# Row pair nine of a decoder layer's second down product as seven block products, and one exchange split eight and eight

## The chip, the cores and the metric

The kernel runs on one core of a Trainium2 chip. The metric is device time in microseconds (us). A core has a matrix engine (TensorE, PE in the profile, with its weight loads as PEld), VectorE (DVE), ScalarE (ACT), GpSimd (POOL) and a sync engine (SP) that only starts transfers. Each engine works through its own queue in order, and the queues wait for each other by semaphores.

## The reference

One layer of a decoder trunk, 256 positions, model width 1024, feed-forward width 2816, all in float32:

```python
h = x + 0.5 * swiglu(rms_norm(x), w_gate1, w_up1, w_down1)
h = h + hybrid_mixer(rms_norm(h), ...)
h = h + 0.5 * swiglu(rms_norm(h), w_gate2, w_up2, w_down2)
out = rms_norm(h)

def swiglu(x, w_gate, w_up, w_down):
    return (jax.nn.silu(x @ w_gate) * (x @ w_up)) @ w_down
```

The mixer projects to queries, keys, values and gates, runs two kinds of attention, gates, merges and projects back. The change touches the last product of each `swiglu` (the down product) and the step from the first feed-forward to the mixer.

## The kernel before

**Products.** Every large product is split into a rounded high part and a rest: `wh`, `wl` for weights, `hth`, `htl` and the like for activations. A unit (line 360) is three matmuls, high times high, high times `wl`, rest times high, of 128x512 outputs each, that gather in one PSUM bank (`mm3`, lines 354 to 358). After each unit one tick of a list of waiting work runs (`Weave`, from line 101), and then `W.pump` (line 229) may issue one further weight split: ScalarE casts to `wh` (L214, or L218 with a gain), VectorE subtracts to `wl` (L215, L219). The raw weights come in 512 KB transfers of two tiles each, issued by SP, into four slots (`load`, line 171); a slot's next transfer is issued after the split that reads it last.

**Lead of the splits.** During a down product `W.ahead` is 9 and ten pairs `wh`, `wl` exist. So beside product number i stands, in the queues, the split of product i + 8. I count products of the second down product from 0 at its first row pair.

**The down product.** The hidden rows, 2816 long, make 22 blocks of 128, and so eleven row pairs. A plain pair (two blocks, two column halves of the weights, two token halves) has four weight tiles and eight units. For pairs one, three, five and seven (`SEVEN`, g = 0, 2, 4, 6) seven block products stand in place of the eight. `seven()` (from line 654) issues them, and they need

- four sums of weight tiles (`T`, `seventh`, line 196, VectorE) beside three raw tiles, so seven splits in place of four;
- four sums of hidden blocks (`cs`, lines 561 to 564, VectorE), split to `c` (a cast on ScalarE, a subtraction on VectorE). `turn_hidden` (line 549) issues these after the exchange that turns the hidden rows around;
- shared results X, Y, Z, V in two two-bank tiles of PSUM beside the blocks' own banks. Once the last such pair is done, `post()` (line 673) adds combinations of them to h: seven operations on VectorE (L677, L683, L685, L689, L694) and a copy on ScalarE (L681). In the code before it is added to the list after pair seven, with a delay of three ticks.

In the second feed-forward the first nine pairs are the head, over all four result blocks; block (1,1) has its own bank. Then the list is flushed, the residual of block (1,1) is added to h, and the tail runs the last four blocks of rows for result block (0,0), (0,1), (1,0) and (1,1), this one in two pieces of 256 columns. After each follows a residual (L650) and a part of the last normalization (`finish`, line 1164: squares L393 on ScalarE, products with the final gain L1177 and L1185, small steps L1181 to L1193 on VectorE and ScalarE, and the output transfers). So the order on all engines is written out by hand here (`ordered`, from block 3 of the second feed-forward on). Between the end of the first down product's head and that place, only TensorE and SP follow the written order, and a planner orders ScalarE, VectorE and GpSimd.

**The exchange of u.** After the first feed-forward's residual of the left half of h, `moved` (line 428) turns it for token half t: VectorE transposes 32x32 blocks (L432), 16 transfers exchange blocks (`exchange`, L510), and after some ticks ScalarE and VectorE split the result to `uh` and `ul` (L387, L388), which the first projection multiplies. The transfers go in turn to three entries, GpSimd, SP, GpSimd, so eleven are on GpSimd and five on SP, three per tick. Between them SP issues weight transfers. GpSimd also computes the row factors of the norm (L403 to L410) behind them.

Of the kernel before, what the change touches and what calls it, by code (L numbers as in the profile page):

```python
# [21 lines left out]
KD = D // P  # L22
FB = FF // 256
KF = FF // P
# [3 lines left out]
NEG = -1e30  # L28
CH = 2
N_TILES = 376  # L30
SEVEN = (0, 2, 4, 6)
W_DOWN = 2 * KF + 3 * len(SEVEN)
W_IN = FB * KD + W_DOWN
W_BR = W_IN + 10 * KD
W_OUT = W_BR + 16
W_FFN2 = W_OUT + 2 * KD
# [101 lines left out]
def _items():  # L138

    out, n = [], 0  # L140

    def plain(count):
        nonlocal n
        out.extend((n + i, None) for i in range(count))
        n += count

    for f in range(2):
        plain(FB * KD)
        for g in range(KF // 2):
            if g in SEVEN:  # L150
                out.extend((n, j) for j in range(7))
                n += 4
            else:
                plain(4)
        if f == 0:
            plain(W_FFN2 - W_IN)
    assert n == N_TILES
    return out
# [88 lines left out]
def hybrid_layer_kernel(ctx, tc, x, xt, pos, g_final, bgate, wstream, out):  # L247
    nc = tc.nc
# [18 lines left out]
    def big(nm, dt=F32R):  # L267
        return work.tile([P, 1024], dt, name=nm, tag="big", bufs=24)

    def wide(nm, w=768):  # L270
        return work.tile([P, w], F32, name=nm, tag="f", bufs=4)
# [9 lines left out]
    first = consts.tile([P, 3 * KD + T], F32, name="first")  # L281
# [3 lines left out]
    def gain(i):  # L285
        for n, (lo, hi) in enumerate(((0, FB * KD), (W_IN, W_BR), (W_FFN2, W_FFN2 + FB * KD))):
            if lo <= i < hi:
                k = (i - lo) % KD
                if n == 0 and i < 2 * KD:
                    k = i // 2  # L290
                if n == 2 and i - lo < 3 * KD:
                    k = (i - lo) // 12 * 4 + (i - lo) % 4
                return gk[:, n * KD + k:n * KD + k + 1]
        return None

    W = Weights(nc, wpool, lambda nm: big(nm, F32), row512, wstream, gain, WB, AHEAD0)
# [57 lines left out]
    def mm3(o, ah, al, w, first, last):  # L354
        wh, wl = w
        nc.tensor.matmul(o, ah, wh, start=first, stop=False)  # L356
        nc.tensor.matmul(o, ah, wl, start=False, stop=False)  # L357
        nc.tensor.matmul(o, al, wh, start=False, stop=last)  # L358

    def unit(o, a, w, first, last):  # L360
        mm3(o, a[0], a[1], w, first, last)
        weave.tick()
        W.pump()
# [48 lines left out]
    class Normed:  # L412
# [15 lines left out]
        def moved(self, c):  # L428

            s = slice(c * 512, c * 512 + 512)  # L430
            q = big(f"{self.nm}q{self.t}{c}", F32)
            nc.vector.transpose(slots(q[:, 0:512], 4), plain(h[self.t][:, s]))  # L432
            yield D_SQUARES
            queues = [nc.gpsimd, nc.sync, nc.gpsimd] if self.nm == "u" else [nc.sync, nc.gpsimd]
            yield from exchange(q[:, 512:1024], q[:, 0:512], 4, queues, 1)
            yield D_EIGHT
            split(plain(self.parts[0][:, s]), plain(self.parts[1][:, s]), slots(q[:, 512:1024], 4))
            self.there.add(c)
# [59 lines left out]
    def slots(q, n):  # L498

        return q[:, 0:n * P].rearrange("p (g s w) -> p s g w", g=4, s=n)  # L500

    def plain(q):
        return q.rearrange("p (s g w) -> p s g w", g=4, w=32)

    def exchange(moved, squares, n, queues, gap):

        w = 32
        for m in range(16):
            i, j = divmod(m, 4)
            queues[m % len(queues)].dma_start(moved[j * w:j * w + w, i * n * w:(i + 1) * n * w],  # L510
                                              squares[i * w:i * w + w, j * n * w:(j + 1) * n * w])
            if m % len(queues) == len(queues) - 1:
                yield gap
# [14 lines left out]
    def ffn(base, xn, nm, on_half, lag, last=False):  # L528


        hts, crossed = {}, {}
        squares = {}

        def hidden(b, t, bank):
            sh = wide(f"sh_{nm}{b}_{t}", 512)
# [13 lines left out]
        def turn_hidden(p, n):  # L549
            moved = big(f"hm_{nm}{p}", F32)  # L550
            yield from exchange(moved, squares[p], n, [nc.gpsimd if p > 3 else nc.sync], D_MOVE)
            yield D_MOVED
            hts[p] = big(f"hth_{nm}{p}"), big(f"htl_{nm}{p}")
            split(plain(hts[p][0][:, 0:n * P]), plain(hts[p][1][:, 0:n * P]), slots(moved, n))
            for g in range(2 * p, 2 * p + 2):
                if g in SEVEN:
                    a11, a21, a12, a22 = (slots(moved, n)[:, g % 2 * 4 + s] for s in range(4))
                    yield D_SUMS
                    raw = wide(f"cs_{nm}{g}", 512)
                    s1, s3, s2, s4 = (plain(raw)[:, s] for s in range(4))  # L560
                    nc.vector.tensor_add(s1, a21, a22)
                    nc.vector.tensor_sub(s3, a11, a21)
                    nc.vector.tensor_sub(s2, s1, a11)
                    nc.vector.tensor_sub(s4, a12, s2)
                    yield D_SUMS
                    both = big(f"c_{nm}{g}")
                    split(both[:, 0:512], both[:, 512:1024], raw)
                    crossed[g] = [[both[:, q * 512 + m * P:q * 512 + (m + 1) * P] for q in range(2)] for m in range(4)]

        for b in range(FB):  # L570
# [5 lines left out]
            if b == 0 and lag == 0:  # L576
                pairs = [two_banks(f"gu_{nm}{c}") for c in range(2)]
                os = [[pair[:, t * 512:t * 512 + 512] for t in range(2)] for pair in pairs]
                for i in range(2 * KD):
                    k, c = divmod(i, 2)  # L580
# [25 lines left out]
            for t, k in lagged(KD, 2) if b > (2 if lag else 1) else ():  # L606
                if k == 0:
                    banks[t] = acc_bank(f"gu_{nm}{b}_{t}")
                i = base + b * KD + k
# [9 lines left out]
        def out_bank(t, c):  # L619
            if (t, c) not in banks:  # L620
                if (t, c) != (1, 1):
                    banks[t, c] = acc_bank(f"dn_{nm}{t}{c}")
                else:
                    banks[t, c] = y_bank(f"dn_{nm}{t}{c}")
            return banks[t, c]

        def down(t, c, k, i, piece=None):

            o = k % 4 * 256 + t * P
            ht = [q[:, o:o + P] for q in hts[k // 4]]  # L630
            w = W.get(i)
            if piece is not None:
                if k == head:
                    banks[piece] = two_banks(f"dn_{nm}p{piece}")
                cols = slice(piece * 256, piece * 256 + 256)
                mm3(banks[piece][:, 0:256], *ht, [q[:, cols] for q in w], k == head, k == KF - 1)
                weave.tick()
                W.pump()
            else:
                first = (t, c) not in started  # L640
                started.add((t, c))
                unit(out_bank(t, c), ht, w, first, k == (head - 1 if last and (t, c) == (1, 1) else KF - 1))

        def residual(t, c, piece=None):
            if piece is None:
# [6 lines left out]
        common, started = {}, set()  # L652

        def seven(g, i):

            def blk(k, t):
                o = k % 4 * 256 + t * P
                return [q[:, o:o + P] for q in hts[k // 4]]

            if not common:  # L660
                for pair in ("XY", "ZV"):
                    both = two_banks(f"dn_{nm}{pair}")
                    common.update(zip(pair, (both[:, 0:512], both[:, 512:1024])))
            s1, s3, s2, s4 = crossed[g]
            for o, a in (("X", blk(2 * g, 0)), ((0, 0), blk(2 * g + 1, 0)), ((0, 1), s4),
                         ("V", s1), ("Z", s3), ("Y", s2), ((1, 0), blk(2 * g + 1, 1))):
                shared, first = o in common, o not in started
                started.add(o)
                unit(common[o] if shared else out_bank(*o), a, W.get(i), first, shared and g == SEVEN[-1])
                W.done(i)  # L670
                i += 1

# [24 lines left out]

        tail = TAILS[2 if last else 1]
        head = KF - tail
        i = base  # L700
        W.ahead = AHEAD_DOWN
        for k in range(head):
            if k // 2 in SEVEN:
                if k % 2:
                    seven(k // 2, i)
                    i += 7
                    if k // 2 == SEVEN[-1]:
                        weave.add(post(), D_POST)
                continue
            for c in range(2):  # L710
                for t in range(2):
                    down(t, c, k, i)
                W.done(i)
                i += 1
# [8 lines left out]
        for t, c in ((0, 0), (0, 1), (1, 0), (1, 1)) if last else ((0, 0), (1, 0), (0, 1), (1, 1)):  # L723
            pieces = (0, 1) if last and (t, c) == (1, 1) else (None,)
            for piece in pieces:
                for k in range(head, KF):
                    i = base + c * tail + k - head
# [118 lines left out]
    def project(bi, evac):  # L846
        banks = {}
        for t, k in lagged(KD, KD if bi == 0 else 2):
            if k == 0:
                banks[t] = acc_bank(f"in{bi}_{t}")  # L850
            i = W_IN + bi * KD + k
            unit(banks[t], un[t].blk(k), W.get(i), k == 0, k == KD - 1)
# [193 lines left out]
    a, b, ys = {}, {}, {}  # L1046
# [52 lines left out]
    for c in range(2):  # L1099
        banks = {}  # L1100
        for t, k in lagged(4, 2):
            if k == 0:
                banks[t] = acc_bank(f"ba{t}{c}")
            i = W_BR + c * 4 + k
# [28 lines left out]
    for t in range(2):  # L1133
        for c in range(2):
            ps = acc_bank(f"bb{t}{c}")
            for k in range(4):
                i = W_BR + 8 + c * 4 + k
# [8 lines left out]
    for c in range(2):  # L1146
        s = slice(c * 512, c * 512 + 512)
        for t in range(2):
            ps = acc_bank(f"wo{t}{c}")
            for k in range(KD):  # L1150
                i = W_OUT + c * KD + k
# [105 lines left out]
```

## Time and profile before

| what | us |
|---|---|
| three runs, median (lowest to highest) | 548.54 (548.23 to 549.52) |
| the profiled execution, its own time | 549.75 |
| its span from first to last instruction | 548.0 |
| TensorE's granted clock, mean | 0.997 of full |
| first matmul of the second down product | 484.15 |
| last matmul | 541.30 |

Busy times of engines are shares of that span; a matmul's end is modelled, so the distance between starts, not the length, tells what one costs. In the timeline a row gives start, length, engine, line, operation, output and inputs, and in brackets an idle time before it and what ended it.

### The profile page before, as it was taken

To read this page: it belongs to the slowest core of one execution; us is meant where nothing else is said; L and a number is where in the kernel's file an instruction comes from. 1 tells how busy PE (TensorE), PEld (TensorE's weight loads), DVE (VectorE), ACT (ScalarE), POOL (GpSimd) and SP (SyncE) were. 2 spreads that over 40 slices of the span, in tenths; PEclk is the share of its full clock that TensorE was granted. 3 is DMA by queue.
4 is the path that set the end of the run, shared out by engine and by line. 5 is a ranking of instruction groups with operands and counts; after the bars stand their busy time and mean duration, and the time that the engine had idled before them with its cause. 6 is when DMAs were issued, how large, how long until landed. Compare 5 with 4: busy or idle time off the path is not lost.

```text
span 548.0 us, 8036 instructions
## 1 busy us (share of the span) xinstructions
PE 539.8 (99%) x2466; PEld 445.2 (81%) x2466; DVE 451.9 (82%) x803; ACT 357.2 (65%) x612; POOL 111.7 (20%) x226
## 2 busy tenths in 40 slices
PE   9999999999999999999999999999999999999995
PEld 6888888888888788888888888888888888888884
DVE  5797799889999666889888888877777878899985
ACT  6775666657754766677876675456666566667643
POOL 2400000036103656032022200274000000253000
PEclk9999999999999999999999999999999999999998
DMA  8956766685766766445555354677667666758532
GB/s 284 405 190 220 241 208 201 210 255 173 232 213 203 251 203 218 156 154 177 181 162 173 116 201 145 206 244 239 216 199 223 224 213 217 226 168 257 200 112 77
DMA packets 42603, 112.23 MB, mean 205 GB/s; under 512 B 8352, under 2 KB 15936, under 8 KB 42560
## 3 DMA queue, kind: packets, MB, share of 16 engines
q1 hardware_dynamic: 37632, 106.49, 58.8%
q0 software_dynamic: 4496, 4.56, 3.1%
q10 hardware_dynamic: 432, 0.67, 0.4%
q8 instruction: 19, 0.31, 0.2%
q14 instruction: 24, 0.20, 0.1%
HBM read 102.25 MB, written 1.05 MB: 188 GB/s over the span
## 4 chain that ended last, share of the span: by engine, by line
PE 91%; DVE 3%; DMA 2%; issue 1%; ACT 1%; SPq 0%; POOL 0%; ACTq 0%; DVEq 0%
PE gu_f L356 13%; PE gu_f L358 13%; PE gu_f L357 13%; PE in L356 7%; PE in L358 6%; PE in L357 6%; PE dn_f L358 4%; PE dn_f L356 4%; PE dn_f L357 4%; DVE wl L215 1%; PE wo L356 1%; PE wo L358 1%; PE wo L357 1%; PE gu_f L369 1%; DMA uq<-uq 1%
## 5 line engine op out<-in xcount | busy, mean ns | idle before, releaser
L219 DVE SCALAR_TENSOR_TENSOR wl<-raw,first,wh 128x512 fp32r<-128x512 f32 (+1 forms) x257 | 182.6, 743 | 33.2 <-ACT wh L218 32.5
L218 ACT ACTIVATE wh<-raw,first 128x512 fp32r<-128x512 f32 (+1 forms) x257 | 173.4, 716 | 50.0 <-PE gu_f L358 24.9
L214 ACT CAST wh<-raw 128x512 fp32r<-128x512 f32 x112 | 64.9, 619 | 22.2 <-PE bb L358 5.5
L215 DVE TENSOR_TENSOR wl<-raw,wh 128x512 fp32r<-128x512 f32 x112 | 73.8, 690 | 3.9 <-ACT wh L214 3.7
L510 POOL DMA_DIRECT2D hm_f<-hs_f x64 | 31.6, 501 | 205.5 <-DMA hm_f<-hs_f 101.5
L358 PE MATMUL gu_f<-wh,zl 128*128 128x512 f32 x176 | 68.5, 389 | 0.0
L356 PE MATMUL gu_f<-wh,zh 128*128 128x512 f32 x176 | 68.5, 389 | 0.0
L357 PE MATMUL gu_f<-wl,zh 128*128 128x512 f32 x176 | 68.5, 389 | 0.0
L356 PE MATMUL in<-wh,uh 128*128 128x512 f32 x160 | 63.7, 398 | 0.4 <-ACT uh L387 0.4
L358 PE MATMUL in<-wh,ul 128*128 128x512 f32 x160 | 62.7, 392 | 0.0
L357 PE MATMUL in<-wl,uh 128*128 128x512 f32 x160 | 62.5, 391 | 0.0
L356 PE MATMUL gu_f<-wh,xh 128*128 128x512 f32 x144 | 56.1, 389 | 0.0
L357 PE MATMUL gu_f<-wl,xh 128*128 128x512 f32 x144 | 56.1, 389 | 0.0
L358 PE MATMUL gu_f<-wh,xl 128*128 128x512 f32 x144 | 56.0, 389 | 0.0
L356 PE MATMUL dn_f<-wh,hth_f 128*128 128x512 f32 x124 | 48.4, 390 | 0.0
L358 PE MATMUL dn_f<-wh,htl_f 128*128 128x512 f32 x124 | 48.3, 389 | 0.0
L357 PE MATMUL dn_f<-wl,hth_f 128*128 128x512 f32 x124 | 48.3, 389 | 0.0
L358 PEld LDWEIGHTS gu_f<-wh,zl 128*128 128x128 f32 x176 | 33.0, 188 | 6.9
L356 PEld LDWEIGHTS gu_f<-wh,zh 128*128 128x128 f32 x176 | 33.0, 188 | 6.9
L357 PEld LDWEIGHTS gu_f<-wl,zh 128*128 128x128 f32 x176 | 33.1, 188 | 6.8
L358 PEld LDWEIGHTS in<-wh,ul 128*128 128x128 f32 x160 | 30.0, 188 | 6.9 <-DVE ul L388 0.4
L356 PEld LDWEIGHTS in<-wh,uh 128*128 128x128 f32 x160 | 30.1, 188 | 6.5 <-ACT uh L387 0.8
(320 smaller groups left out, 955.6 us busy)
## 6 DMA issues: line engine op xcount, KB each, us to landing
raw<-in_wstream SPq DMA_DIRECT2D x185, 512.0 KB, 4.3
hm_f<-hs_f SPq DMA_DIRECT2D x128, 32.0 KB, 3.9
raw<-in_wstream SPq DMA_DIRECT2D x5, 256.0 KB, 5.2
h<-in_x SPq DMA_DIRECT2D x2, 512.0 KB, 8.2
hm_f<-hs_f POOLq DMA_DIRECT2D x32, 32.0 KB, 3.6
bg<-in_bgate POOLq DMA_DIRECT2D x4, 256.0 KB, 4.5
xin<-in_xt SPq DMA_DIRECT2D x2, 256.0 KB, 6.3
hm_f<-hs_f POOLq DMA_DIRECT2D x32, 16.0 KB, 4.0
```

The lines of the kernel that those rows point to most:

```text
L214: self.nc.scalar.copy(hi, raw)
L215: self.nc.vector.tensor_sub(lo, raw, hi.bitcast(F32))
L218: self.nc.scalar.activation(hi[:, s], raw[:, s], AF.Copy, scale=g)
L219: self.nc.vector.scalar_tensor_tensor(lo[:, s], raw[:, s], g, hi[:, s].bitcast(F32), op0=ALU.mult, op1=ALU.subtract)
L356: nc.tensor.matmul(o, ah, wh, start=first, stop=False)
L357: nc.tensor.matmul(o, ah, wl, start=False, stop=False)
L358: nc.tensor.matmul(o, al, wh, start=False, stop=last)
L369: nc.tensor.matmul(o, ah, wh, start=first, stop=False)
L510: queues[m % len(queues)].dma_start(moved[j * w:j * w + w, i * n * w:(i + 1) * n * w], squares[i * w:i * w + w, j * n * w:(j + 1) * n * w])
```

## The change

The list of pairs with seven products becomes one list per feed-forward, and pair nine (g = 8) joins it in the second. The names that depend on it follow: `post()` is added after pair nine there, the shared banks' last matmul lies there, and the last matmul into block (1,1)'s own bank is that of pair eight (`behind`). And for u the transfers of the second token half (t = 1) go in turn to SP and GpSimd, eight each, two per tick; those of the first half stay as they were.

```diff
-SEVEN = (0, 2, 4, 6)
-W_DOWN = 2 * KF + 3 * len(SEVEN)
-W_IN = FB * KD + W_DOWN
+SEVENS = (0, 2, 4, 6), (0, 2, 4, 6, 8)
+W_IN = FB * KD + 2 * KF + 3 * len(SEVENS[0])
...
-            queues = [nc.gpsimd, nc.sync, nc.gpsimd] if self.nm == "u" else [nc.sync, nc.gpsimd]
+            queues = [nc.gpsimd, nc.sync, nc.gpsimd] if self.nm == "u" and self.t == 0 else [nc.sync, nc.gpsimd]
...
+        sevens = SEVENS[1 if last else 0]
...
-                if g in SEVEN:
+                if g in sevens:
...
-                unit(out_bank(t, c), ht, w, first, k == (head - 1 if last and (t, c) == (1, 1) else KF - 1))
+                unit(out_bank(t, c), ht, w, first, k == (behind if last and (t, c) == (1, 1) else KF - 1))
...
-                unit(common[o] if shared else out_bank(*o), a, W.get(i), first, shared and g == SEVEN[-1])
+                unit(common[o] if shared else out_bank(*o), a, W.get(i), first, shared and g == sevens[-1])
...
+        behind = max(k for k in range(head) if k // 2 not in sevens)
...
-            if k // 2 in SEVEN:
+            if k // 2 in sevens:
                 if k % 2:
                     seven(k // 2, i)
                     i += 7
-                    if k // 2 == SEVEN[-1]:
+                    if k // 2 == sevens[-1]:
                         weave.add(post(), D_POST)
```

More of the change, by code (lines that the diff above doesn't have):

```diff
@@ L149, in _items @@
         for g in range(KF // 2):
-            if g in SEVEN:
+            if g in SEVENS[f]:
                 out.extend((n, j) for j in range(7))
@@ L555, in turn_hidden @@
             for g in range(2 * p, 2 * p + 2):
-                if g in SEVEN:
+                if g in sevens:
                     a11, a21, a12, a22 = (slots(moved, n)[:, g % 2 * 4 + s] for s in range(4))
```

## The prediction

> **What bounds the kernel now.** The page comes first, its busy times and its chain of work that ended last.
>
> ```profile
> PE 539.8 (99%) x2466; PEld 445.2 (81%) x2466; DVE 451.9 (82%) x803; ACT 357.2 (65%) x612; POOL 111.7 (20%) x226
> ...
> PE 91%; DVE 3%; DMA 2%; issue 1%; ACT 1%; SPq 0%; POOL 0%; ACTq 0%; DVEq 0%
> ```
>
> Over the whole span TensorE sets the time. The change sits in two short stages, so I read these apart, with the table of windows over the second down product: pairs five and six, seven and eight, nine, and the tail.
>
> ```profile
> 504.55:514.75 10.20, 10.20 (x46) 8.45 (x45) 10.20 (x17) 7.22 (x13) 0.00 (x0) 1.00 0.63 216
> 514.75:524.95 10.20, 10.20 (x46) 8.45 (x45) 9.03 (x16) 6.95 (x14) 0.00 (x0) 1.00 0.69 233
> 524.95:530.40 5.45, 5.45 (x26) 4.51 (x25) 5.42 (x10) 4.14 (x6) 0.00 (x0) 1.00 0.12 50
> 530.40:541.30 10.90, 10.90 (x60) 9.50 (x59) 8.28 (x18) 3.91 (x11) 0.00 (x0) 1.00 0.11 41
> ```
>
> The columns after the length are PE, PEld, DVE, ACT and POOL busy. VectorE (DVE) is as full as TensorE: 10.20 of 10.20 us, 5.42 of 5.45 in pair nine. It still has 10.90 - 8.28 = 2.62 us free in the tail. Its waits from 522 us to the end say where its room lies:
>
> ```profile
> DVE h L650 <- PE dn_f L358: 2.0, 1, 2.0
> DVE wl L215 <- ACT wh L214: 1.2, 1, 1.2
> ...
> DVE h L650 <- PE dn_f2p L358: 0.3, 1, 0.3
> ```
>
> So 2.0 + 1.2 + 0.3 = 3.5 us is all that VectorE can take in before it, and not TensorE, ends the kernel. What the change asks of it is the question.
>
> **The end: TensorE's side.** PE rows of the timeline, first matmul of pair nine, first of the tail, last of all:
>
> ```profile
> 524.95 0.39 PE L356 MATMUL dn_f<-wh,hth_f 128*128 128x512 f32 x1
> ...
> 530.39 0.39 PE L356 MATMUL dn_f<-wh,hth_f 128*128 128x512 f32 x1
> ...
> 541.30 0.28 PE L358 MATMUL dn_f2p<-wh,htl_f 128*128 128x256 f32 x1
> ```
>
> Pair nine's eight products take 530.39 - 524.95 = 5.44 us, 0.68 each. Seven take 4.76, so TensorE would finish 0.68 us earlier.
>
> **The end: VectorE's side.** In this stage the order is written by hand, and the rows of VectorE's timeline show what it costs:
>
> ```profile
> 486.35 0.28 DVE L561 TENSOR_TENSOR cs_f<-hm_f 128x128 f32<-128x128 f32 x1
> ...
> 487.28 1.28 DVE L215 TENSOR_TENSOR wl<-raw,wh 128x512 fp32r<-128x512 f32 x2
> 488.48 0.68 DVE L388 TENSOR_TENSOR c_f<-cs_f,c_f 128x512 fp32r<-128x512 f32 x1
> ...
> 518.51 3.70 DVE L215 TENSOR_TENSOR wl<-raw,wh 128x512 fp32r<-128x512 f32 x6
> 522.12 0.69 DVE L677 SCALAR_TENSOR_TENSOR h<-dn_f2XY,h 128x512 f32<-128x512 f32 x1
> ...
> 524.60 0.68 DVE L683 TENSOR_TENSOR xy_f<-dn_f2XY,xs_f 128x512 f32<-128x512 f32 x1
> 525.31 0.69 DVE L685 TENSOR_TENSOR xyz_f<-dn_f2ZV,xy_f 128x512 f32<-128x512 f32 x1
> 525.92 0.68 DVE L215 TENSOR_TENSOR wl<-raw,wh 128x512 fp32r<-128x512 f32 x1
> ...
> 532.53 1.47 DVE L650 SCALAR_TENSOR_TENSOR h<-dn_f,h 128x512 f32<-128x512 f32 x2
> 536.03 0.69 DVE L650 SCALAR_TENSOR_TENSOR h<-dn_f,h 128x512 f32<-128x512 f32 x1 [2.03 <-PE dn_f L358]
> 536.64 0.14 DVE L1181 TENSOR_SCALAR fin<-fin 128x1 f32<-128x1 f32 x1
> ...
> 539.18 0.69 DVE L650 SCALAR_TENSOR_TENSOR h<-dn_f,h 128x512 f32<-128x512 f32 x1
> 540.18 0.42 DVE L650 SCALAR_TENSOR_TENSOR h<-dn_f2p,h 128x256 f32<-128x256 f32 x1 [0.32 <-PE dn_f2p L358]
> 540.53 1.02 DVE L1177 TENSOR_TENSOR hg<-h,gB 128x512 f32<-128x512 f32 x2
> 541.62 0.42 DVE L650 SCALAR_TENSOR_TENSOR h<-dn_f2p,h 128x256 f32<-128x256 f32 x1
> ```
>
> Six operations from 518.51 to 522.12: one starts every 0.60 us, although each lasts 0.69. That pitch is the price. An operation that needs the result just before it starts 0.71 later (524.60 to 525.31). Reading PSUM costs no more: 525.31 to 525.92.
>
> The Trainium skill, Perfetto Trace Analysis, section Optimizing Scalar/DVE Operations, gives about 60 ns of overhead on SBUF and 125 on PSUM. By it five PSUM readers would add an estimated 0.3 us to the sum; the row just read does not agree.
>
> Added for pair nine: four weight sums (T, line 196) and three more wl, 7 x 0.60 = 4.2 us. For its crossed blocks four small sums, 487.28 - 486.35 = 0.93, and one c_f subtraction at the pitch, 0.60. Together 5.73 us. All of it stands ahead of the additions to h.
>
> The additions also move. The split of product i+8 is issued beside product i. post() used to begin in the third unit of pair eight, and its eight operations filled in between splits. Now it is added after the last unit of pair nine, when the splits of all eight tail weights have been issued, and the flush issues it whole. So VectorE's queue, with products counted from 0 at pair one, runs thus:
>
> - crossed blocks of nine: before pair seven's T, since h of pair nine lands there; everything after shifts by 1.53, and wl 43 goes from 518.51 to 520.04.
> - T, wl, four times over, from 520.64; wl 48 at 525.45; wl 49 to 58 until 532.06.
> - add(0,0) at 532.06 (before 522.12: +9.94).
>
> The rest of post depends on ScalarE's copy xs, and the final sums on its squares:
>
> ```profile
> 522.85 0.59 ACT L681 COPY xs_f<-dn_f2XY 128x512 f32<-128x512 f32 x1 [1.50 <-DVE h L677]
> ...
> 534.04 0.63 ACT L393 ACTIVATE sq_fin<-h 128x512 bf16<-128x512 f32 x1 [4.19 <-DVE h L650]
> 534.58 0.19 ACT L393 ACTIVATION_READ_ACCUMULATOR sq_fin<-h 128x1 f32 x1
> ```
>
> xs starts 0.73 after add(0,0), lasts 0.59: xy at 532.06 + 0.73 + 0.59 + 0.06 = 533.44. Six steps follow, four at 0.71 and two at 0.60: xyz 534.15, h(1,0) 534.86, xyv 535.46, h(0,1) 536.17, xyzv 536.77, h(1,1) 537.48. Then the residuals: (1,1) 538.19, (0,0) 538.79, (0,1) 539.39. The last stood at 536.03 and waited 2.03 us for TensorE; now it is 3.36 late and TensorE's block has long been there.
>
> Next is line 1181, which needs the square of (0,0). That was done 534.77 - 534.04 = 0.73 after its start, far ahead. Now it starts at 539.53 and is read at 540.3, so 1181 goes from 536.64 to 540.3: +3.66. The row's end work keeps that shift to residual (1,0), 539.18 to 542.84. Piece 0 follows 0.60 later (before: 1.0, with its wait), at 543.44. Its own 0.35 and the two hg products, 0.95, put the last piece at 544.75 to 544.85, against 541.62. That is **+3.15 us**, and what follows it is unchanged. The saved 0.68 vanishes: TensorE would end at 540.9, four us earlier than VectorE gets to its last block.
>
> Does TensorE starve on the way? Tightest is product 39: wl 39 stood five pitches ahead of the x6, at 515.5, and moves by 1.53 to 517.0, ready 517.7; TensorE wants it in its second matmul, nine products less a matmul ahead of 524.95, at 519.06. Product 50's wl is ready at 527.3 against 529.26, product 51's at 527.9 against 529.94. The tail's last weight pair takes the slot freed by pair nine's last T:
>
> ```profile
> DMA to landing us min/median/max: 3.2/4.4/5.3
> ```
>
> Freed 524.9, landed 529.3 (at most 530.2), cast 0.62 later, wanted by wl 57 at 530.86: nothing, at worst 0.1 us. The other slots come earlier. Other engines: ScalarE's four more casts, 0.62 each, lie in its spare 2.98 of 10.20 us. TensorE's pieces of block (1,1) need the banks that post reads; xy has read the first by 534.1, xyzv the second by 537.5, ahead of the pieces at about 537.9 and 539.3. The edit that closes block (1,1) after pair eight issues nothing. One tile more in the rotation of large buffers takes over tiles read long before. The count of weight loads stays.
>
> Bounds of this part: were there no latency between dependent steps and squares, only the work that finds no room would count, 5.73 - 3.5 = +2.2. If each of some ten dependent or cross-engine steps took 0.1 us more, +4.1. I take 3.15, which the rows give step by step.
>
> **The u transfers.** TensorE's only wait after the start, and what it waits for:
>
> ```profile
> PE in L356 <- ACT uh L387: 0.4, 1, 0.4
> ...
> 188.78 0.39 PE L358 MATMUL in<-wh,ul 128*128 128x512 f32 x1
> ...
> 190.66 0.39 PE L356 MATMUL in<-wh,uh 128*128 128x512 f32 x1
> ...
> 178.25 3.91 POOL L510 DMA_DIRECT2D uq<-uq  x8 [0.28 <-DVE wl L219]
> ...
> 184.89 0.50 POOL L510 DMA_DIRECT2D uq<-uq  x1 [0.60 <-DMA uq<-uq]
> ...
> 178.78 2.40 SPq L510 DMA_DIRECT2D uq<-uq  x4
> 181.28 12.14 SPq L182 DMA_DIRECT2D raw<-in_wstream  x5
> ...
> 188.93 0.62 ACT L387 CAST uh<-uq 128x512 fp32r<-128x512 f32 x1 [2.34 <-issue]
> ...
> 189.57 0.69 DVE L388 TENSOR_TENSOR ul<-uq,uh 128x512 fp32r<-128x512 f32 x1 [2.20 <-DMA raw<-in_wstream]
> ```
>
> Four matmuls from 188.78 to 190.66 take 1.88 us; at 0.227 each (5.44 / 24) they take 0.91: **0.97 us** lost. POOL issues eight of the second half, then waits for landings of earlier ones; the last goes out at 184.89, and the cast comes 4.04 later. With eight on POOL, the last starts about 181.7, with no wait. SP gets three more at 0.6 each (2.40 / 4) behind its last: 181.2, 181.8, and, a weight load between, about 182.9. At the same 4.04, uh starts at 187.0. To lose nothing it must start by 188.1 (ul follows 0.64 later, lasts 0.69, wanted 189.46). So I take the whole 0.97. If a landing on SP were 2 us slower under the weight traffic, nothing is won; if the later split met a bad place in ScalarE's queue, 0.5 is lost; ScalarE is idle 2.34 us there. The weight loads pushed back 1.2 to 1.8 us feed casts well later than 188, behind a wait for buffers. Since TensorE waits for nothing from 190.66 to 541.30, the 0.97 passes to the end, both queues shifting alike.
>
> **Sum.** Span 548.0 + 3.15 - 0.97 = 550.2; with the 1.75 us around it the profiled run, 549.75, becomes 551.9. The runs' median is 548.54, 1.2 below that run: 548.54 + 2.18 = **550.7**.
>
> **Rivals.**
>
> *TensorE still sets the end.* The saved unit counts, if VectorE had slack: 548.54 - 0.68 - 0.97 = 546.9. For it: PE 99%, and the chain is 91% PE. Against it: 10.20 of 10.20. It decides if VectorE's added work before the tail stays under about 3.5 us; I count 5.73 plus moved dependences. The Trainium skill, Perfetto Trace Analysis, section Identifying the Most-Contended Engine, warns that matmul busy time is no good measure and asks for LDWEIGHTS busy; by that rule VectorE (82%) stands ahead of PEld (81%), which speaks against this change, and the windows agree more strongly (10.20 against 8.45).
>
> *The room takes up all it can.* Dependent steps hide in the tail, and only the lower bound is left: 2.2 - 0.97 = +1.2, 549.8. For it: the tail's free 2.62 us. Against it: the dependent 0.71 of the rows.
>
> *VectorE ends it, and the transfers win nothing*: +3.15, 551.7. SP is a single queue with weight loads ahead.
>
> **How the numbers follow.** Forecast 0.62, TensorE-bound 0.09, room taken up 0.14, no win from transfers 0.15. The forecast's own spread is about 0.6 either way. Since ScalarE's and VectorE's order between the two feed-forwards is planned, not written, add half a microsecond. 549.4 to 552.0 holds the forecast, the last rival, and the one on the room. About 0.3% (1.65 us) is what a measurement here can tell from no change: slower beyond 550.2 has most of the forecast and all of the last rival, 0.72; within, 0.20; faster, 0.08, from the TensorE-bound case.
>
> **What would show it.** Right: add(0,0) near 531 (532.06 - 0.97) with seven VectorE operations behind it and no split between; the wait of 2.0 us for PE gone; TensorE's last matmul near 539.65 and VectorE's last piece near 543.8; POOL's u issues without waits after the first eleven, uh near 187, no gap at 189. Wrong: the last piece still released by TensorE, or gaps in VectorE's row between 505 and 532; a new wait on SP ahead of the last u transfer.

## The result, and the profile after

| | before | after |
|---|---|---|
| median of six runs each on one chip, us | 548.39 (548.11 to 549.52) | 552.32 (552.06 to 552.43) |
| the profiled execution, its own time | 549.75 | 552.16 |
| its span | 548.0 | 550.5 |

The ratio is 1.0067, with a 95% interval of 1.0054 to 1.0080: the change costs 3.9 us of the median. The direction and the mechanism of pair nine were forecast; the size forecast was 2.2, and 552.32 lies above the range's 552.0.

The two spans differ by 2.5 us only, the two medians by 3.9. That alone says that the profiled execution of before doesn't stand for the median as the one of after does; it comes back below.

The page of after, busy times and chain of work that ended last:

```profile
PE 538.4 (98%) x2463; PEld 444.3 (81%) x2463; DVE 458.1 (83%) x815; ACT 359.2 (65%) x616; POOL 113.1 (21%) x223
...
PE 92%; DVE 5%; ACT 1%; issue 1%; DVEq 0%; ACTq 0%
```

Three matmuls fewer (one unit), 12 VectorE operations more, 6.2 us more on VectorE, and VectorE's share of the chain goes from 3% to 5%. Over the whole span it still looks like a kernel that TensorE sets. The table of windows shows more (length, then PE, PEld, DVE, ACT and POOL busy), for pair nine and the tail:

```profile
523.60:528.40 4.80, 4.80 (x23) 3.97 (x22) 4.80 (x10) 4.29 (x9) 0.00 (x0) 1.00 0.59 189
528.40:539.30 10.90, 10.90 (x61) 9.50 (x59) 9.88 (x18) 3.49 (x7) 0.00 (x0) 1.00 0.00 0
```

Pair nine is 4.80 us long where it was 5.45, and in the tail VectorE is now busy 9.88 of 10.90 us where it was 8.28. Its waits from 505 us to the end are led by two short ones for ScalarE:

```profile
DVE xy_f L683 <- ACT xs_f L681: 0.7, 1, 0.7
DVE fin L408 <- ACT fin L1188: 0.3, 1, 0.3
```

The 2.0 us for TensorE, the 1.2 for ScalarE's cast and the 0.3 for the last piece are all gone: the whole room of 3.5 us is used up. The timeline of after, TensorE's last row among VectorE's:

```profile
519.31 0.68 DVE L195 TENSOR_TENSOR T<-raw 128x512 f32<-128x512 f32 x1
...
525.93 4.90 DVE L214 TENSOR_TENSOR wl<-raw,wh 128x512 fp32r<-128x512 f32 x8
...
530.75 0.68 DVE L677 SCALAR_TENSOR_TENSOR h<-dn_f2XY,h 128x512 f32<-128x512 f32 x1
...
532.09 0.69 DVE L683 TENSOR_TENSOR xy_f<-dn_f2XY,xs_f 128x512 f32<-128x512 f32 x1 [0.65 <-ACT xs_f L681]
...
536.20 0.69 DVE L677 SCALAR_TENSOR_TENSOR h<-xyzv_f,h 128x512 f32<-128x512 f32 x1
...
536.93 1.89 DVE L650 SCALAR_TENSOR_TENSOR h<-dn_f,h 128x512 f32<-128x512 f32 x3
...
539.00 0.15 DVE L1182 TENSOR_SCALAR fin<-fin 128x1 f32<-128x1 f32 x1 [0.19 <-ACT sq_fin L392]
...
539.28 0.28 PE L357 MATMUL dn_f2p<-wh,htl_f 128*128 128x256 f32 x1
...
543.42 0.42 DVE L650 SCALAR_TENSOR_TENSOR h<-dn_f2p,h 128x256 f32<-128x256 f32 x1
```

add(0,0), the first of `post()`, stands at 530.75, behind all eight tail splits. `post()` has eight operations on VectorE (four additions to h, four combinations), not seven as said above. The three residuals run back to back without a wait. TensorE has its last matmul at 539.28; VectorE takes up the last piece 4.14 us later (before: 541.62 - 541.30 = 0.32). From 530.75 on, VectorE's queue and the steps inside it are the kernel's end.

**Where the time went, by the two traces.** I set the starts of the same matmuls side by side. TensorE of after is 0.65 us ahead from the first big product on, 1.61 ahead after the gap at 189, 1.35 ahead from 266 on, and so 1.35 ahead at pair nine. There it saves 0.68 (541.30 - 1.35 - 0.68 = 539.27, measured 539.28). VectorE's last piece stands at 543.42 - 541.62 = +1.80. Without the 1.35 that came from earlier stages this is **+3.15 us**, the term that the prediction worked out.

The 0.65 at the start comes from first weights that arrived sooner in this execution, in code that the change doesn't touch. The rows are the first big product's matmul, in the timeline of before and of after:

```profile
8.42 0.50 PE L369 MATMUL gu_f<-wh,xh 128*128 128x512 f32 x1 [0.31 <-ACT wh L218]
```
```profile
7.78 0.50 PE L368 MATMUL gu_f<-wh,xh 128*128 128x512 f32 x1
```

The u transfers, in the timeline of after, did as forecast:

```profile
177.72 3.92 POOL L509 DMA_DIRECT2D uq<-uq  x8 [0.36 <-DVE wl L218]
...
183.26 0.51 SPq L509 DMA_DIRECT2D uq<-uq  x1
...
187.13 0.62 ACT L386 CAST uh<-uq 128x512 fp32r<-128x512 f32 x1 [0.72 <-DMA raw<-in_wstream]
```

GpSimd issues its eight without a wait for landings, SP's last follows at 183.26, the cast starts at 187.13 (forecast 187.0), and TensorE waits for nothing there. But the 0.25 us given back at 266, in the attention products named y_a, was not foreseen. The waits of the weight loads there, of before and of after:

```profile
PEld y_a L946 <- DVE pl L388: 0.3, 1, 0.3
```
```profile
PEld y_a L947 <- DVE pl L387: 0.6, 1, 0.6
```

This loss comes with the new order of the transfers. From one y_a matmul to the next (255.46 to 266.18 in before) pass 10.71 to 10.74 us in all ten profiles of this document that have the old order, and 10.91 to 11.01 in the four that have the new one. By which path the transfers reach it was not followed.

And one more loss stands after everything that was forecast. In the trace's records the last bytes of the output land at 548.80, and SP, which ends the program, is through with its waits at 549.62: 0.82 us. Before, the two stand at 547.01 and 547.18: 0.16. So **0.65 us** are lost in SP's waits. What these waits are is worked out below. The view of SP's waits, of before and of after, shows only that SP now stands 0.4 us longer at an output:

```profile
SPq L1253 <- DMA out<-o: 1.8, 2, 1.2
```
```profile
SPq L1254 <- DMA out<-o: 2.2, 2, 1.6
```

Two questions are left. **Was the 0.97 us gap at 189 something that every execution of before has,** and that the change wins? Then VectorE and the end cost 4.9 in the median. Or did it belong to the one profiled execution? Then VectorE's 3.15 and SP's 0.65 are nearly the 3.9. And **what sets the end:** the amount of VectorE's work, its order, or SP's waits?

### The profile page after: what moved, and what is told of

Read it like the earlier page. It is cut to its first block, busy times and chain, and to the rows that moved or that the text cites. A ratio compares the mean times of both kernels' runs of the same rounds, so it can differ in the third digit from the quotient of the medians.

```text
span 550.5 us, 8049 instructions
## 1 busy us (share of the span) xinstructions
PE 538.4 (98%) x2463; PEld 444.3 (81%) x2463; DVE 458.1 (83%) x815; ACT 359.2 (65%) x616; POOL 113.1 (21%) x223
## 4 chain that ended last, share of the span: by engine, by line
PE 92%; DVE 5%; ACT 1%; issue 1%; DVEq 0%; ACTq 0%
PE gu_f L355 13%; PE gu_f L357 13%; PE gu_f L356 13%; PE in L355 6%; PE in L357 6%; PE in L356 6%; PE dn_f L357 4%; PE dn_f L355 4%; PE dn_f L356 4%; DVE wl L214 1%; PE wo L355 1%; PE wo L357 1%; PE wo L356 1%; PE gu_f L368 1%; PE gu_f L369 1%; PE gu_f L371 1%
## 5 line engine op out<-in xcount | busy, mean ns | idle before, releaser
L355 PE MATMUL dn_f<-wh,hth_f 128*128 128x512 f32 x118 | 46.0, 390 | 0.0
L357 PE MATMUL dn_f<-wh,htl_f 128*128 128x512 f32 x118 | 45.9, 389 | 0.0
L356 PE MATMUL dn_f<-wl,hth_f 128*128 128x512 f32 x118 | 45.9, 389 | 0.0
```

## The experiments

Times are medians in us beside the kernel before on the same chip (548.48, 548.54 and 548.44 in the three sets). "Before" in a diff is the kernel before, "after" the changed one.

**before_again**: the kernel before, unchanged, profiled once more.

> The kernel before, unchanged, profiled once more. Theory 1 (the first profile is a usual execution, and all of its 0.97 us gap ahead of the second u half is there each time): span near 548.0 and the gap there again. Theory 2 (the first profile was a slow execution, by some 1.3 us against its own median of 548.39): span near 546.7, with the first weights landing as early as in the changed kernel (-0.63) and part of the gap at 189 us missing. Time 548.4 in both.

548.53; profiled run 548.69, span 547.0. Timeline around the gap:

```profile
183.79 0.50 POOL L510 DMA_DIRECT2D uq<-uq  x1 [0.60 <-DMA uq<-uq]
...
187.90 0.62 ACT L387 CAST uh<-uq 128x512 fp32r<-128x512 f32 x1 [1.52 <-issue]
...
188.90 0.39 PE L356 MATMUL in<-wh,uh 128*128 128x512 f32 x1
...
190.77 0.39 PE L358 MATMUL in<-wh,ul 128*128 128x512 f32 x1
```

GpSimd waits for the same landing as in the first profile, but its last transfer goes out at 183.79 and not at 184.89, and the cast starts at 187.90, ahead of the 188.1 that the prediction gave as the latest without loss. From 188.90 to 190.77 TensorE starts eight matmuls further, 1.87 us; at 0.227 each that is 1.82. All but 0.05 us of the gap is gone. The first profile's execution was 1.36 us slower than the median of its kernel (549.75 against 548.39), and its gap was part of that.

The gap isn't in that one execution alone, though. The runs below bring eight more profiles with the old order of the transfers. TensorE's waits in one of them, dose4, from 20 us on:

```profile
PE in L359 <- ACT uh L390: 0.4, 1, 0.4
```

By the starts of its matmuls dose4 loses 0.9 us there, and its profiled execution (549.24) is 0.7 above its median. Of the ten profiles, two lose 0.9 to 1.0 us at this place, three lose 0.3 to 0.5 (no_sums, no_sums2, nine_pool), and five less than 0.1. The four with the new order lose nothing. So the change does remove a loss, but one that shows in full only in some executions: about 0.2 us in the middle of the ten.

**u_only**: before, with the u transfers of the second half eight and eight.

```diff
-queues = [nc.gpsimd, nc.sync, nc.gpsimd] if self.nm == "u" else [nc.sync, nc.gpsimd]
+queues = [nc.gpsimd, nc.sync, nc.gpsimd] if self.nm == "u" and self.t == 0 else [nc.sync, nc.gpsimd]
```

> Only the u transfers eight and eight. Theory 1: the gap's 0.97 us is won, 0.25 of it is given back at the first attention pair, and 0.65 us is added at the end, where SP waits for its semaphores in a fixed order and the last output's one now stands early in it: -0.97 + 0.25 + 0.65 = -0.1, 548.3. Theory 2: the gap is mostly not there in usual executions, so only the 0.65 at the end shows: +0.4 to +0.8, 548.8 to 549.2. Rival: the three transfers more on SP delay something else, over +1.0.

549.19, ratio 1.0014 (1.0005 to 1.0022): this part wins nothing; it costs 0.7 us. The parts are 0.65 at the end and 0.25 at y_a, less the 0.2 or so that the usual gap is worth. Its waits on SP at the end:

```profile
SPq L1253 <- DMA out<-o: 2.2, 2, 1.6
```

The same longer wait as in after, in a kernel whose last stage is untouched.

**nine_only**: after, without the new order of the u transfers.

> Only pair nine as seven products; the u transfers as before. Theory: VectorE's queue ends the kernel 3.15 us later against TensorE's clock, and the end waits of SP are in the old order: 548.4 + 3.15 = 551.5. Rival (TensorE sets the end): 547.7. Rival (the whole 3.9 us of the change comes from pair nine): 552.3.

551.46, ratio 1.0055 (1.0043 to 1.0068): +2.98. The last wait on SP is that of before, and the end of VectorE's queue that of after:

```profile
SPq L1254 <- DMA out<-o: 1.8, 2, 1.2
```
```profile
525.81 4.90 DVE L214 TENSOR_TENSOR wl<-raw,wh 128x512 fp32r<-128x512 f32 x8
530.63 0.68 DVE L677 SCALAR_TENSOR_TENSOR h<-dn_f2XY,h 128x512 f32<-128x512 f32 x1
```

The two parts add up: 2.98 + 0.71 = 3.69 against 3.9 for both, within what such medians can tell.

**What the last 0.65 us are.** At its end SP waits for the semaphores of the transfers, two at a time, in an order that is the same in all seven profiles of the table below. This is worked out from the trace's records of SP's instructions, not shown in a view of the profile. The last waits of after (each starts once its semaphores are there; start in us, semaphore numbers):

```
548.180  wait 100, 115
548.818  wait 102, 114      <- the last output landed at 548.80, on 102
548.888  wait 104, 113
549.266  wait 105, 112
549.355  wait 106, 111
549.419  wait 108, 101
549.487  wait 109, 103
549.551  wait 110, 107
549.619  through
```

Each costs about 0.07 us; one cost 0.38, in u_only too, and why is open. The transfers of SP and ScalarE take their semaphores in turn from eight. The change starts three more on SP (383, before 380), so the last outputs move on by three places: from 108 and 109, near the end of that order, to 100 and 102. From the last output's own wait on there are now seven waits to go through, where before there were two.

| kernel | transfers on SP | semaphores of the last two outputs | last landing | SP through | between |
|---|---|---|---|---|---|
| before | 380 | 108, 109 | 547.01 | 547.18 | 0.16 |
| before_again | 380 | 108, 109 | 545.97 | 546.14 | 0.17 |
| u_only | 383 | 100, 102 | 545.80 | 546.61 | 0.81 |
| nine_only | 380 | 108, 109 | 548.67 | 548.84 | 0.17 |
| after | 383 | 100, 102 | 548.80 | 549.62 | 0.82 |
| after_sems | 388 | 108, 109 | 550.02 | 550.16 | 0.14 |
| after_moved | 380 | 108, 109 | 549.20 | 549.36 | 0.16 |

**after_sems**: after, with five tiny loads on SP ahead of the second feed-forward's fourth block, so that the count comes round to the same places.

```diff
+for e in range(5):
+    nc.sync.dma_start(cos[:, 0, 2 * e:2 * e + 2].bitcast(I32), pos)
```

> The changed kernel with five more 1 KB transfers on SP in the second feed-forward (8 bytes per row into a dead tile), so that the eight semaphores of the SP and ScalarE transfers stand at the end as they stood before. Theory (SP's waits behind the last output in a fixed order cost 0.65 us): 552.3 - 0.65 = 551.7, and the time from the last landing to SP's last drain falls from 0.82 to 0.16 us. Rival (the end is longer for another reason): 552.3 or, by the five transfers, more.

552.46, not faster than after; a miss. The wait after the last landing is as short as forecast, but 15 of the 16 parts of the last output had landed by 549.27, and one came at 550.02. On that DMA engine the trace shows an 8 KB instruction fetch at 548.85 between the last pieces of output. In before the fetch comes at 547.42 and in after at 549.90, behind the outputs; presumably the five added instructions moved it ahead of them. So the run took one cause away and set another one in its place, and it settles nothing by its time.

**after_moved**: after, with three transfers of the first feed-forward's first exchange given from SP to GpSimd, so that SP starts 380 again.

```diff
+back = {5, 8, 11} if p == 0 and not last else ()
...
-queues[m % len(queues)].dma_start(...)
+(nc.gpsimd if m in back else queues[m % len(queues)]).dma_start(...)
```

> The changed kernel with three of the 16 transfers of the first feed-forward's first exchange put from SP to GpSimd, so that SP starts 380 transfers as before the change and no instruction is added. Theory (0.65 us of the change are SP's end waits, whose order follows from the count of SP's transfers): last landing to SP's last drain back to 0.16 us from 0.82, time 552.4 - 0.65 = 551.7. Rival (the count does not matter): 552.4, and the 0.82 stays.

551.80, ratio 1.0058 (1.0045 to 1.0070); 0.5 us less than after's 552.32, where 0.65 was expected, with nothing changed near the end, and the short wait on SP:

```profile
SPq L1255 <- DMA out<-o: 1.8, 2, 1.2
```

So the place of the last semaphore shows in the time both ways: u_only puts it early in the order and loses 0.7 (with y_a's 0.25 in it), after_moved puts it back and wins 0.5.

**Is it VectorE's amount of work?** First less of it. **no_sums**: nine_only without pair nine's four sums; raw tiles stand in their places.

```diff
+if s < N_TILES - 12:
+    self.nc.vector.tensor_sub(self.made[o], self.tile(s + a), b)
...
+if s >= N_TILES - 12:
+    return self.tile(s + (0, 2, 3, 0, 1, 2, 3)[j]), {4: s // CH, 6: s // CH + 1}.get(j)
```

> Pair nine only (u transfers as before), and the four weight sums of pair nine left out: raw tiles stand in their place, so its products are not those of the reference. Theory (VectorE's queue sets the end): four operations of 0.60 less, 551.46 - 2.4 = 549.1. Rival (TensorE or the moved additions set it, not the amount of VectorE's work): 551.4.

550.89, a miss by 1.8. The waits of ScalarE, and of VectorE for ScalarE, say why:

```profile
ACT wh L216 <- DMA raw<-in_wstream: 2.8, 4, 1.2
...
DVE wl L217 <- ACT wh L216: 1.4, 2, 0.9
```

The raw tiles were held for three splits longer (the slots go after the fifth and seventh, not the second and fourth), the next weights landed later, and casts and splits waited for them; VectorE's 1.4 us of waits stand against the 1.8 missed. The edit had taken work away and put a wait in. **no_sums2** lets the weights go when nine_only does, and splits a resident tile (the final gain) in place of the four sums, which are left out:

```diff
+if s >= N_TILES - 12 and j > 2:
+    raw = self.spare
...
+W.spare = gB[:, 0:512]
```

> As the kernel without sums, but with a resident tile of the final gain in place of the sums, so that no weight slot is held longer than in the pair-nine kernel; the products of pair nine are not the reference's. Theory (VectorE's amount of work sets the end; the kernel without sums was held back by weight slots released two splits later): 551.46 - 2.4 = 549.1, without waits of ScalarE's casts for raw weights. Rival (the weight stream is the next limit there in any case): 550.5 to 550.9.

549.32, ratio 1.0009 (1.0000 to 1.0018): 2.14 us less than nine_only, for four operations at 0.60. Its profiled execution (550.18) is 0.86 above the median, and VectorE still waits 0.5 us there for a late cast. Timeline:

```profile
529.43 0.68 DVE L680 SCALAR_TENSOR_TENSOR h<-dn_f2XY,h 128x512 f32<-128x512 f32 x1
...
542.09 0.41 DVE L653 SCALAR_TENSOR_TENSOR h<-dn_f2p,h 128x256 f32<-128x256 f32 x1
```

Pair nine still has seven products and its additions still stand in the last rows; only VectorE's four sums are gone, and more than two thirds of the loss with them. So it is the amount of work, not the place of the additions, that costs most.

Then more of it, in the kernel before. **dose4** puts four unused subtractions, 4 x 0.60 = 2.4 us, among the splits ahead of the tail:

```diff
+n = len(self.items) - i
+for q in range(1 if 9 <= n <= 12 else 0):
+    self.nc.vector.tensor_sub(self.sums(f"D{i}_{q}"), raw, hi.bitcast(F32))
```

> The kernel before, with four more 128x512 subtractions on VectorE in pair nine, whose results nobody reads. Theory (2.0 + 1.2 + 0.3 = 3.5 us of room): 4 x 0.60 = 2.4 us are taken in, 548.5. Rival (no room, VectorE sets the end already): +2.4, 550.9.

548.52, ratio 1.0002 (0.9993 to 1.0011): no loss at all. VectorE's waits from 503 to the end:

```profile
DVE wl L215 <- ACT wh L214: 1.2, 1, 1.2
DVE fin L412 <- ACT fin L1190: 0.3, 1, 0.3
```

The 2.0 and 0.3 us of waits for TensorE have gone, and the time stays. So 2.4 us of the room are taken in without a trace in the time. The 1.2 us for ScalarE's cast are still there: that part of the 3.5 this run does not test.

**dose10** does the same with two for each of five splits, 6.0 us (`range(2 if 9 <= n <= 13 else 0)`).

> The kernel before, with ten more such subtractions in the last split of pair eight and in pair nine. Theory: 6.0 - 3.5 = +2.5, 551.0. Rival (TensorE sets the end whatever VectorE does): 548.5.

552.18, +3.7, more than expected. The wait that sets it is another one:

```profile
PE dn_f L360 <- DVE wl L215: 2.2, 3, 0.8
```
```profile
PEld dn_f L360 <- DVE wl L215: 3.8, 4, 1.3
```

TensorE waited for late splits; beside before_again its rows fall from 0.13 us behind at 530.9 to 4.08 at 534.1. Past the room, extra VectorE work hits TensorE itself when it stands ahead of the splits that TensorE wants next. In after TensorE waits for nothing in this stage: there `post()`'s eight operations on VectorE stand behind the last split, not between the splits.

**Can the loss be avoided?** Three tries, all without the u part. **nine_pool** gives pair nine's four sums to GpSimd:

```diff
-self.nc.vector.tensor_sub(self.made[o], self.tile(s + a), b)
+(self.nc.gpsimd if s >= N_TILES - 12 else self.nc.vector).tensor_sub(self.made[o], self.tile(s + a), b)
```

> Pair nine only, its four weight sums on GpSimd instead of VectorE, all results kept. Theory: VectorE gets 2.4 us less, 551.46 - 2.4 = 549.1, if a sum on GpSimd takes up to some 1.5 us, since its queue is empty there from 502 us on. Rival (the sums on GpSimd come late or slow VectorE down): 550 to 552.

554.56, ratio 1.0103: 3.1 us more than nine_only, a miss. Timeline of GpSimd and VectorE:

```profile
515.29 7.69 POOL L195 TENSOR_TENSOR T<-raw 128x512 f32<-128x512 f32 x1 [14.22 <-DVE wl L214]
...
519.34 2.50 DVE L214 TENSOR_TENSOR wl<-raw,wh 128x512 fp32r<-128x512 f32 x4
...
522.95 1.29 POOL L195 TENSOR_TENSOR T<-raw,raw 128x512 f32<-128x512 f32 x1
...
523.67 5.34 DVE L214 TENSOR_TENSOR wl<-T,wh 128x512 fp32r<-128x512 f32 x4 [1.84 <-ACT wh L213]
```

The first sum lasts from 515.29 to 522.98. VectorE works back to back until 519.34 + 2.50 = 521.84; the sum ends 1.14 us later, about what the next one takes alone (1.29). So it seems to have stood until VectorE paused, as far as the rough spans of GpSimd in a profile can tell. And VectorE's four splits beside the later sums take 5.34 us, not 4 x 0.60. The Trainium skill, SBUF — State Buffer, section Who interferes with whom, says that a VectorE instruction with two SBUF inputs contends with a GpSimd instruction that reads SBUF, and that the ports which the two share are an exclusive lock. The rows agree, with the first sum's 7.69 us and the splits' 5.34; and by them GpSimd was kept out not for one such instruction but over a whole run of them.

**nine_pool2** gives the four `cs` sums and the `c` subtraction of pair nine to GpSimd too:

```diff
+side = nc.gpsimd if g == 8 else nc.vector
-nc.vector.tensor_add(s1, a21, a22)
+side.tensor_add(s1, a21, a22)
...
-split(both[:, 0:512], both[:, 512:1024], raw)
+split(both[:, 0:512], both[:, 512:1024], raw, rest=side)
```

> As the one before, and pair nine's four sums of hidden blocks and its c_f subtraction on GpSimd too. Theory: VectorE's added work falls from 5.73 to 1.8 us, under the 3.5 us of room, and TensorE sets the end with one unit less: 548.48 - 0.68 + about 0.3 for the dependent additions = 547.8 to 548.4. Rival (the moved additions alone keep VectorE late): 548.7 to 549.5.

555.79, ratio 1.0131, worse again. Timeline:

```profile
500.79 10.79 POOL L562 TENSOR_TENSOR cs_f<-hm_f 128x128 f32<-128x128 f32 x1
...
510.58 0.68 DVE L195 TENSOR_TENSOR T<-raw,T 128x512 f32<-128x512 f32 x1
...
511.55 0.46 POOL L563 TENSOR_TENSOR cs_f<-hm_f 128x128 f32<-128x128 f32 x1
```

The same picture on a tile a quarter as wide: 10.79 us, ending 0.3 after VectorE's last operation in a row (510.58 + 0.68), and 0.46 for the next.

**nine_early** runs pair nine ahead of pair eight, so that `post()` can again fill in between splits:

```diff
-for g in range(KF // 2):
+for g in (range(KF // 2), (0, 1, 2, 3, 4, 5, 6, 8, 7, 9, 10))[f]:
...
-for k in range(head):
+for k in [*range(14), 16, 17, 14, 15] if last else range(head):
```

> Pair nine only, but put ahead of pair eight (weight tiles in that order), so that the additions to h start in the third unit of pair eight and stand between splits, as before the change. Theory: VectorE's 5.73 us less 3.5 us of room stay, and the 0.9 us of the moved additions go: 548.5 + 2.2 = 550.7. Rival (their place costs nothing): 551.5. Rival (two pairs of seven in a row starve TensorE for longer than its 3 us of slack): over 552.

552.75, ratio 1.0078: a miss by 2 us, and within the last rival's range. The waits of TensorE, and of VectorE for ScalarE:

```profile
PE dn_f2ZV L356 <- DVE wl L214: 0.8, 1, 0.8
PE dn_f L356 <- DVE wl L214: 0.6, 1, 0.6
...
DVE wl L214 <- ACT wh L213: 1.5, 2, 1.2
```

Two seven-product pairs in a row ask for fourteen splits and eight sums at once, and VectorE can't keep up: TensorE waits for `wl`. But that isn't what ends the kernel. VectorE's last piece still stands last, at 544.43 against 543.28 in nine_only, and VectorE now waits 1.5 us for late casts, one of them behind 2.0 us in which ScalarE waits for raw weights. How much each of these costs was not taken apart. No version here beats the kernel before.

## Why the prediction was right where it was, and wrong where it was not

**What bounds: right.** Reading VectorE by stage (10.20 of 10.20 us busy) and its room from its waits (3.5 us) was the step that carried the forecast. dose4 shows most of this room on the chip: 2.4 us of work for nothing.

**VectorE's side: right, to a tenth in the traces.** +3.15 forecast, 3.15 in the two traces, 2.98 (2.4 to 3.7) in the medians of nine_only. add(0,0) was forecast at 532.06 on the clock of before; less the 1.35 by which this trace runs ahead that is 530.71, and it stands at 530.75. The steps behind it hold too: the small step after the square of (0,0) was forecast at 540.3, and 539.00 + 1.35 is 540.35. So this term isn't luck. TensorE's saved 0.68 is there and vanishes. The rival in which the room takes all but 2.2 falls, as 2.98 is above it; the one in which TensorE sets the end falls by sign.

**The u transfers: wrong.** The step that failed is "So I take the whole 0.97", with the sum that takes it off "548.54 + 2.18". The gap was real in its trace, its cause was read rightly, and the change removes it. But the sum was put on the median of the runs, and a usual execution loses about 0.2 there, not 0.97: of ten profiles with the old order only two lose that much. And the new order costs 0.25 at y_a, which the prediction put at nothing, so that u_only wins nothing. The prediction even had the numbers for doubt: that execution was 1.2 us slower than the median, and its only wait was this one. The rival "the transfers win nothing", 551.7, was nearer for this part, but it has no loss in it either.

**SP's end: not in the prediction.** "What follows it is unchanged" failed by 0.65 us. The prediction counted the three transfers that SP gets as 0.6 us each in SP's queue at 181, and not as places in the turn of semaphores that SP waits for at the end. u_only and after_moved show the cost.

**The sum.** 3.15 + 0.65 at the end + 0.25 at y_a - 0.2 for the usual gap = 3.85 against 3.9 measured; forecast 3.15 - 0.97 = 2.18. Of the 1.7 us missed, about 0.8 is the gap, 0.65 SP's end and 0.25 y_a. That it comes out so closely is partly luck, since the medians don't tell a tenth or two. Why the first weights landed 0.65 us sooner in one execution than in the other was not tried; in before_again the first big product is 0.11 ahead of before, in dose4 0.51, so it differs between executions of the same code.

## What to carry to other kernels

Before trading TensorE work for work on another engine, read that engine's waits in the stage itself: their sum is the most that it can take in, whatever the engine's share of the span is. Work past it costs its length and more, for dependent steps and late splits come on top: here 2.2 us past the room cost 3.0, and 2.5 cost 3.7. A short wait seen in one profiled execution, above all in one slower than the median, comes off a median only by the share of executions that have it, so count it in several profiles. And where the number of transfers on a queue changes, look at what the program does after its last landing: the place in the order of the last waits can cost more than the edit wins.

## What the runs showed that was not expected

- Three transfers more on SP, 360 us before the end, lengthen the end by 0.65 us, through the semaphore on which the last output lands (0.16 to 0.17 us from landing to the end of SP's waits on one place, 0.81 to 0.82 on the other).
- A GpSimd subtraction of 128x512 that takes 1.29 us took 7.69 beside VectorE working back to back, and a sum of 128x128 took 10.79 where the next took 0.46.
- In one trace (after_sems) an 8 KB instruction fetch stood between the last pieces of output, and the part behind it landed 0.75 us after the other fifteen (549.27 to 550.02). That the fetch is the cause is inferred.
- Two profiled executions of one kernel stood 1.0 us apart in their spans (548.0 and 547.0), 0.9 of it by one gap that only the slower one has; of ten profiles with the same code there, two have it in full.
